# A Mamba-2 and attention layer on one core: y's norm taken for two chunks of the scan together

## Chip, cores and metric

One core of a Trainium2 chip runs the whole layer. The metric is the device time in microseconds; the time given is the median of several runs.

## What is computed

One encoder layer with two branches over 512 tokens of width 2048. After an RMSNorm and one input projection, branch A is a convolution and a bidirectional chunked state-space scan, whose result y is gated and normed in four groups of 512 columns. Branch B is attention with compressed queries and keys. Both are projected, gated, summed and projected out. Cut to what the change touches:

```python
y_fwd = ssd_scan(xs, dtf, a_f, bm, cm)                     # chunks of 128 tokens
y_bwd = flip(ssd_scan(flip(xs), flip(dtb), a_b, flip(bm), flip(cm)))
y = (y_fwd + y_bwd + d_skip[:, None] * xs)
y = y.reshape(b, s, D_SSM) * jax.nn.silu(z_ssm)
y = rmsnorm(y.reshape(b, s, SSM_GROUPS, D_SSM // SSM_GROUPS),
            ssm_norm_w.reshape(SSM_GROUPS, D_SSM // SSM_GROUPS)).reshape(b, s, D_SSM)
```

So each token has, for each of the four groups g, one root mean square over 512 columns. A chunk c is 128 tokens, one per partition; a group's chunk is a tile of 128 x 512, and its norm needs one number per partition.

## The kernel before

The kernel is one program in stages: the input's norm and transposes, the gate products (Strassen's scheme, `wz`, `wgs`, `wga`), the scan, the attention heads, and the projections. Large matmuls are done three times with fp32r halves (`mm3`, L168): a weight chunk of 128 x 1024 is loaded by SyncE (`wraw`), ScalarE (ACT) makes its high half `wh` (L164), VectorE (DVE) its low half `wl` (L165), and TensorE (PE) runs 24 matmuls from it.

The scan is `ssd_group(g)` (L1034), called for g = 0 to 3. A group has a **state loop** of three steps (L1141), which makes the running states and the off-diagonal terms `off`, and a **second loop** over four chunks c and two halves q of four heads (L1208), which makes the products within a chunk. In the second loop `seg_make` (L1170) builds the decay products G on DVE (two scans L1177, E L1180, G L1187 and L1188) and on ACT (exponential L1181, scaled copies L1186), and `diag` (L1191) lets PE multiply them into the bank `yb` (L1198). `diag` is called one half later than its G. After the second half of a chunk it adds `yb` to `yo` on DVE (L1201) and calls `y_norm` (L993).

`y_norm` multiplies by the gate z on DVE (L995), sums the squares on ACT (L997), scales the sum on DVE (L998), takes a root on ACT (L186, which needs a table load there), refines its reciprocal with five DVE operations on one column (L188 to L192, in `small_rsqrt`), and scales y by it on ACT (L999). `y_turn` (L1001) then transposes y on PE into a bank `turn` (L1005), which ACT copies out (L1009) and stores to `yn_d`.

Between these steps PE is fed from a queue of other products, `fill`: projections of the next group (`xbc`), of the attention's inputs (`qkv`) and of its gate (`za`). `gap()` (L1072) takes the next share of them, some 30 matmuls in the second loop. PE's order is the order in which the code is written; the other engines' order is set by a scheduler with priorities, and each engine runs its instructions in order. The norm has a raised priority (L1202).

Before the change, a finished chunk is put on a queue `turns`, and one is turned in each second half (q = 1) while more than one is waiting: chunk 0 at c = 2, chunk 1 at c = 3, chunk 2 at the end of the group (L1227) and chunk 3 in the first step of the next group's state loop (L1150), or for the last group after 60 matmuls of fill (L1241).

Of the kernel before, what the change touches and what calls it, by code (L numbers as in the profile page):

```python
# [12 lines left out]
F32 = mybir.dt.float32  # L13
F32R = mybir.dt.float32r
I32 = mybir.dt.int32
AF = mybir.ActivationFunctionType
ALU = mybir.AluOpType
AX = mybir.AxisListType

P = 128  # L20
# [12 lines left out]
EPS = 1e-6  # L33
# [40 lines left out]
def build(tc, a):  # L74
    nc = tc.nc
    act, dve, pool, pe = nc.scalar, nc.vector, nc.gpsimd, nc.tensor
    opened = {}

    def open_pool(name, bufs=1, side="left", **kw):
        cm = tc.tile_pool(name=name, bufs=bufs, side=side, **kw)  # L80
        p = cm.__enter__()
        opened[name] = cm
        return p
# [13 lines left out]
    hi = open_pool("hi", side="right")  # L97
# [4 lines left out]
    def few(n):  # L102

        n_small[0] += n
        assert n_small[0] <= 96
        return small[:, n_small[0] - n:n_small[0]]
# [42 lines left out]
    def pb(n="pb"):  # L149
        return ps.tile([P, SEQ], F32, tag="pb", bufs=2, name=n)  # L150

    def pc(n="pc"):
        return ps.tile([P, SEQ], F32, tag="pc", bufs=1, name=n)
# [29 lines left out]
    def small_rsqrt(v, n, new):  # L183

        t = new("rt")
        act.activation(t, v, AF.Sqrt)  # L186
        r = new("rr")
        dve.reciprocal(r, t)  # L188
        dve.tensor_mul(t, r, r)
        dve.tensor_mul(t, t, v)  # L190
        dve.tensor_scalar(t, t, -0.5, 1.5, ALU.mult, ALU.add)
        dve.tensor_mul(r, r, t)  # L192
        return r
# [12 lines left out]
    for t in range(TT):  # L206
# [3 lines left out]
        for i, cs in enumerate(slice(*e) for e in zip(edges, edges[1:])):  # L210
# [3 lines left out]
            if i == 0:  # L214
                most, v, root, r = (few(1) for _ in range(4))
# [97 lines left out]
    def put(dst, t):  # L313
        act.dma_start(dst, t)
# [113 lines left out]
    fill = Fill()  # L428
# [527 lines left out]
    def tmp2(name, n=SEQ):  # L956
        return sw.tile([P, SEQ], F32, tag="t", bufs=8, name=name)
# [14 lines left out]
    ssz = few(16)  # L972
# [8 lines left out]
                i = qkv_left.pop(0)  # L981
                fill.add("qkv", qkv_gen(i, sq_q if i < 6 else sq_kv, tmp2))

    def rsqrt1(v):

        return small_rsqrt(v, 1, lambda n: hi.tile([P, 1], F32, tag={"rt": "mx", "rr": "nm"}[n], bufs=4, name=n))

    def z_load(c, g):
        z = st("z")
        nc.sync.dma_start(z, zs_d[c][g])  # L990
        return z

    def y_norm(c, g, y, z):  # L993

        dve.tensor_mul(y, y, z)  # L995
        s_ = ssz[:, 4 * c + g:4 * c + g + 1]
        act.activation(z, y, AF.Square, accum_out=s_)  # L997
        dve.tensor_scalar(s_, s_, 1.0 / 512, EPS, ALU.mult, ALU.add)  # L998
        act.activation(y, y, AF.Copy, scale=rsqrt1(s_))  # L999

    def y_turn(c, g, y):  # L1001

        tp = pb("turn")
        for i in range(4):
            pe.transpose(tp[:, i * P:(i + 1) * P], y[:, i * P:(i + 1) * P], ident)  # L1005
        y = tmp2("yt")
        for i in range(4):
            k = 4 * g + i
            act.activation(y[:, i * P:(i + 1) * P], tp[:, i * P:(i + 1) * P], AF.Copy,  # L1009
                           scale=vec[:, V_SN + k:V_SN + k + 1] if g < 2 else vneg[:, k - 8:k - 7])  # L1010
        d = yn_d[f"x{c // 2 + 1}{g // 2 + 1}"].rearrange("p (k t) -> p k t", k=8)
        put(d[:, 4 * (g % 2):4 * (g % 2) + 4, c % 2 * P:(c % 2 + 1) * P], y.rearrange("p (k t) -> p k t", k=4))

    turns = deque()
# [19 lines left out]
    def ssd_group(g):  # L1034
# [37 lines left out]
        def gap():  # L1072
            left[0] += shares.pop(0) * left[1]
            left[0] -= fill.run(left[0])
# [54 lines left out]
        def cb_make(c):  # L1129
            cs = slice(c * P, (c + 1) * P)  # L1130
            cb = pb("cb")
            pe.matmul(cb[:, 0:P], BT[:, cs], CT[:, cs], start=True, stop=True)
            cbf = sw.tile([P, P], F32, tag="cbf", bufs=2, name="cbf")
            cbb = sw.tile([P, P], F32, tag="cbb", bufs=2, name="cbb")
            dve.tensor_mul(cbf, cb[:, 0:P], m_le)
            dve.tensor_mul(cbb, cb[:, 0:P], m_ge)
            cbs[c] = (cbf, cbb)
# [23 lines left out]
        def da_load(c, q):  # L1161
            h0 = g * HPG + q * 4
            das.append([])
            for dd in range(2):
                da = sw.tile([P, 4, P], F32, tag=f"da{dd}", bufs=2, name=f"da{dd}")
                src = da_d[dd, c, h0:h0 + 4].rearrange("h l -> (h l)")
                tc.keep_in_program_order(nc.sync.dma_start(flat(da), src.unsqueeze(0).broadcast_to([P, SEQ])))
                das[-1].append(da)

        def seg_make(c, q):  # L1170

            h0 = g * HPG + q * 4
            sums = []
            for da, mask in zip(das.popleft(), (scan_f, scan_b)):
                with tc.issue_after(put_on[0].ins) if put_on and mask is scan_b else nullcontext():
                    sums.append(tmp2("sum"))
                    dve.tensor_tensor_scan(sums[-1], flat(da), mask, 0.0, ALU.add, ALU.mult)  # L1177
            sf, sb = (t.rearrange("p (h l) -> p h l", h=4) for t in sums)
            E = sw.tile([P, 4, P], F32, tag="E", bufs=2, name="E")
            dve.tensor_add(E, sf, sb[:, :, ::-1])  # L1180
            act.activation(flat(E), flat(E), AF.Exp)  # L1181
            G = sw.tile([P, 4, P], F32, tag="G", bufs=2, name="G")
            cbf, cbb = cbs[c]
            for j in range(4):
                df, db = (dtT[:, c, o + h0 + j:o + h0 + j + 1] for o in (0, NH))
                act.activation(G[:, j], cbf, AF.Copy, scale=df)  # L1186
                dve.scalar_tensor_tensor(G[:, j], cbb, db, G[:, j], ALU.mult, ALU.add)  # L1187
            put_on[:] = [dve.tensor_mul(G, G, E)]  # L1188
            return G

        def diag(c, q, G):  # L1191

            if q == 0:
                ybs[c] = pc("yb")
            yb = ybs[c]
            for j in range(4):
                cs = slice((q * 4 + j) * 64, (q * 4 + j + 1) * 64)
                pe.matmul(yb[:, cs], G[:, j, :], xT[:, c, cs], start=True, stop=True)  # L1198
            if q == 1:
                y = sw.tile([P, SEQ], F32, tag="yz", bufs=2, name="y")  # L1200
                dve.tensor_add(y, yo[:, c], yb)  # L1201
                with tc.high_priority(offset=30):  # L1202
                    y_norm(c, g, y, zs.pop(c))
                turns.append((c, g, y))

        last = None
        da_load(0, 0)
        for c in range(TT):  # L1208
            for q in range(2):
                G = seg_make(c, q)  # L1210
                if q == 0 and c < TT - 1:
                    cb_make(c + 1)
                if (c, q) != (TT - 1, 1):
                    da_load(c + q, 1 - q)
                if q == 1:
                    zs[c] = z_load(c, g)
                gap()
                if q == 1 and len(turns) > 1:
                    y_turn(*turns.popleft())
                if last:  # L1220
                    diag(*last)
                last = (c, q, G)
# [1 line left out]
            loaded[g + 1] = group_loads(g + 1)  # L1224
        gap()
        gap()
        y_turn(*turns.popleft())  # L1227
        diag(*last)

        if g == 2:  # L1230
# [5 lines left out]
    for g in range(GROUPS):  # L1236
        ssd_group(g)
    add_fill("za", len(za_left))
    ahead[0] = 150
    fill.run(60)  # L1240
    y_turn(*turns.popleft())  # L1241
    close_pool("sw")
    close_pool("sp")
# [417 lines left out]
    def w_out(cg, kc):  # L1661
        return w_split(w_load(w_tile("w"), "wo", 0, kc // 4, cg, kc % 4))
# [42 lines left out]
    for cg in range(2):  # L1705
# [4 lines left out]
        for n, kc in enumerate(ORDER):  # L1710
            h, l = w_out(cg, kc)
# [187 lines left out]
```

## Time and profile before

| | |
|---|---|
| median of three runs | 1960.82 us (1956.30, 1960.82, 1961.52) |
| the profiled execution's own time | 1959.01 us |
| its span, first to last instruction | 1957.2 us |
| ScalarE (ACT) busy | 1038.4 us, 53% |
| GpSimd (POOL) busy | 253.0 us, 13% |
| moved by DMA | 383.29 MB, mean 196 GB/s |
| the four groups' second loops, first yb to last yb | about 630 to 691, 757 to 822, 885 to 944, 1011 to 1075 us |

PE is TensorE's matmuls, PEld its weight loads, DVE VectorE, ACT ScalarE, POOL GpSimd, SP SyncE. L12 is line 12 of the kernel before. A row of the timeline gives the start, the duration, the engine and line, the operation, the tiles (output, then inputs), and in brackets how long the engine had been idle before it and what released it. PE's matmuls overlap, so that one that lasts 0.39 us is followed by the next about 0.23 us later.

### The profile page before, as it was taken

Reading aid. Unit: us, or ns where it says so; the run is one execution under the profiler, and the core shown is the slowest. Engines: PE = TensorE matmul, PEld = TensorE weight load, DVE = VectorE, ACT = ScalarE, POOL = GpSimd, SP = SyncE. Lnnn points to the kernel's source line nnn. Section 1 sums busy time; section 2 is a strip of 40 time slices with the busy share of each in tenths; the row PEclk is TensorE's granted clock in tenths of the full one; section 3 lists DMA queues with packets and bytes.
Section 4 is the critical chain, followed back from the end, with each engine's and each line's share of the span. In section 5 each row is a group of like instructions: output and inputs, shape, how many; then the busy total and the mean of one; then the engine's idle time right before and its main releaser. Section 6 shows DMA issues by size and latency. Waiting matters only on the chain.

```text
span 1957.2 us, 24596 instructions
## 1 busy us (share of the span) xinstructions
PE 1931.4 (99%) x8874; PEld 1590.7 (81%) x8874; DVE 1462.0 (75%) x2064; ACT 1038.4 (53%) x1536; POOL 253.0 (13%) x324
## 2 busy tenths in 40 slices
PE   8999999999999999999999999999999999999998
PEld 6878888888888888888888888888877778888886
DVE  7876676776759879789786557676776889879467
ACT  7444445444465856757757444444455355454344
POOL 0011001001112030030210211111021110100011
PEclk9999999999999999999999999999999999999999
DMA  6569669668654545665544867787388787847437
GB/s 218 175 191 261 168 163 249 153 184 240 143 189 151 187 136 166 205 196 182 183 157 142 253 178 209 201 229 193 114 217 305 237 275 282 288 154 242 163 88 169
DMA packets 145306, 383.29 MB, mean 196 GB/s; under 512 B 16608, under 2 KB 34208, under 8 KB 144992
## 3 DMA queue, kind: packets, MB, share of 16 engines
q1 hardware_dynamic: 78240, 232.45, 35.6%
q0 software_dynamic: 31392, 105.40, 23.7%
q10 hardware_dynamic: 35552, 43.87, 6.3%
q8 instruction: 70, 1.15, 0.2%
q14 instruction: 52, 0.43, 0.1%
HBM read 329.55 MB, written 98.17 MB: 219 GB/s over the span
## 4 chain that ended last, share of the span: by engine, by line
PE 80%; DVE 9%; DMA 5%; issue 3%; ACT 2%; POOL 0%; SPq 0%; DVEq 0%; ACTq 0%; POOLq 0%
PE P L630 11%; PE P L631 11%; PE P L629 11%; PE za L169 3%; PE za L171 3%; PE xbc L169 3%; PE za L170 3%; PE xbc L170 3%; PE xbc L171 3%; PE qkv L171 2%; PE qkv L169 1%; PE f L1659 1%; PE f L1658 1%; PE f L1657 1%; PE qkv L170 1%
## 5 line engine op out<-in xcount | busy, mean ns | idle before, releaser
L483 ACT CAST wh<-X 128x1024 fp32r<-128x1024 f32 x164 | 172.5, 1054 | 200.6 <-PE P L631 156.9
L484 DVE TENSOR_TENSOR wl<-X,wh 128x1024 fp32r<-128x1024 f32 x164 | 199.9, 1222 | 88.7 <-ACT wh L483 88.3
L165 DVE TENSOR_TENSOR wl<-wraw,wh 128x1024 fp32r<-128x1024 f32 (+2 forms) x148 | 171.3, 1160 | 81.7 <-ACT wh L164 76.5
L164 ACT CAST wh<-wraw 128x1024 fp32r<-128x1024 f32 (+2 forms) x148 | 142.6, 967 | 113.8 <-PE za L170 31.2
L484 DVE TENSOR_TENSOR wl<-Y,wh 128x1024 fp32r<-128x1024 f32 x88 | 107.5, 1223 | 68.3 <-ACT wh L483 68.3
L483 ACT CAST wh<-Y 128x1024 fp32r<-128x1024 f32 x88 | 92.6, 1054 | 115.5 <-PE P L631 106.5
L169 PE MATMUL xbc<-h_h,wh 128*128 128x512 f32 x384 | 153.1, 399 | 0.0
L171 PE MATMUL xbc<-h_h,wl 128*128 128x512 f32 x384 | 149.9, 390 | 0.0
L170 PE MATMUL xbc<-h_l,wh 128*128 128x512 f32 x384 | 149.5, 389 | 0.0
L629 PE MATMUL P<-wh,h_h 128*128 128x512 f32 x384 | 149.4, 389 | 0.0
L630 PE MATMUL P<-wl,h_h 128*128 128x512 f32 x384 | 149.4, 389 | 0.0
L631 PE MATMUL P<-wh,h_l 128*128 128x512 f32 x384 | 149.4, 389 | 0.0
L483 ACT CAST wh<-wraw 128x1024 fp32r<-128x1024 f32 x68 | 71.7, 1054 | 112.9 <-PE P L631 64.3
L484 DVE TENSOR_TENSOR wl<-wraw,wh 128x1024 fp32r<-128x1024 f32 x68 | 83.1, 1222 | 59.6 <-ACT wh L483 59.4
L630 PE MATMUL P<-wl,S 128*128 128x512 f32 x288 | 112.3, 390 | 0.8 <-DVE wl L484 0.8
L629 PE MATMUL P<-wh,S 128*128 128x512 f32 x288 | 112.1, 389 | 0.2 <-ACT wh L483 0.2
L631 PE MATMUL P<-wh,S 128*128 128x512 f32 x288 | 112.0, 389 | 0.0
L169 PE MATMUL za<-h_h,wh 128*128 128x512 f32 x256 | 101.7, 397 | 0.0
L171 PE MATMUL za<-h_h,wl 128*128 128x512 f32 x256 | 99.9, 390 | 0.0
L170 PE MATMUL za<-h_l,wh 128*128 128x512 f32 x256 | 99.7, 389 | 0.0
L1409 ACT ACTIVATE pr<-s,nm 128x512 f32<-128x512 f32 x64 | 44.1, 689 | 79.4 <-DVE nm L1407 79.4
L171 PEld LDWEIGHTS xbc<-h_h,wl 128*128 128x128 f32 x384 | 72.1, 188 | 15.5
(754 smaller groups left out, 5101.5 us busy)
## 6 DMA issues: line engine op xcount, KB each, us to landing
wraw<-wi SPq DMA_DIRECT2D x102, 512.0 KB, 3.8
T_wps<-wps POOLq DMA_DIRECT2D x32, 512.0 KB, 11.2
da<-da_d SPq DMA_DIRECT2D x64, 256.0 KB, 3.9
T_wpa<-wpa POOLq DMA_DIRECT2D x32, 512.0 KB, 9.7
wraw<-wps SPq DMA_DIRECT2D x24, 512.0 KB, 5.9
wraw<-wo SPq DMA_DIRECT2D x20, 512.0 KB, 3.5
xbc_d<-xbc ACTq DMA_DIRECT2D x24, 256.0 KB, 2.8
wraw<-wun SPq DMA_DIRECT2D x16, 384.0 KB, 5.3
```

What stands on the lines that cost most here:

```text
L164: act.copy(h, raw)
L165: dve.tensor_sub(l, raw, h.bitcast(F32))
L169: pe.matmul(out, wh, xh, start=start, stop=False)
L170: pe.matmul(out, wh, xl, start=False, stop=False)
L171: pe.matmul(out, wl, xh, start=False, stop=stop)
L483: i = act.copy(hi_, raw)
L484: dve.tensor_sub(lo_, raw, hi_.bitcast(F32))
L629: pe.matmul(bs[i], xh, wh, start=(j == 0), stop=False)
L630: pe.matmul(bs[i], xh, wl, start=False, stop=False)
L631: pe.matmul(bs[i], xl, wh, start=False, stop=(j == 7))
L1409: act.activation(pr, s, AF.Exp, bias=nm, scale=SCALE, accum_out=sm_)
L1657: pe.matmul(acc, mh, wh, start=(start and k == 0), stop=False)
```

## The change

The odd chunk's `y_norm` now makes the norm for both chunks of a pair. The sums of squares of a group's chunks lie side by side, the even chunk's `y_norm` ends after its sum, and the odd chunk's takes one root and one set of small operations on two columns for both, then scales both tiles and puts both on `turns`. The small tiles are two fixed pairs of columns (`yr`) and no longer rotating buffers. In the second loop a chunk is turned in each second half when any is waiting, which is chunk 0 at c = 2 and chunk 1 at c = 3 as before. The turn at the end of a group is gone: chunks 2 and 3 are turned in the first and second step of the next group's state loop. For the last group the 60 matmuls of fill are cut into 42 and 18, with a turn after each.

```diff
-    def rsqrt1(v):
-        return small_rsqrt(v, 1, lambda n: hi.tile([P, 1], F32, tag={"rt": "mx", "rr": "nm"}[n], bufs=4, name=n))
+    yr = [few(2), few(2)]
...
+    halves = []
+
     def y_norm(c, g, y, z):
+        s_ = ssz[:, 4 * g + c:4 * g + c + 1]
         dve.tensor_mul(y, y, z)
-        s_ = ssz[:, 4 * c + g:4 * c + g + 1]
         act.activation(z, y, AF.Square, accum_out=s_)
-        dve.tensor_scalar(s_, s_, 1.0 / 512, EPS, ALU.mult, ALU.add)
-        act.activation(y, y, AF.Copy, scale=rsqrt1(s_))
+        halves.append((c, g, y))
+        if c % 2:
+            s2 = ssz[:, 4 * g + c - 1:4 * g + c + 1]
+            dve.tensor_scalar(s2, s2, 1.0 / 512, EPS, ALU.mult, ALU.add)
+            r = small_rsqrt(s2, 2, lambda n: yr[n == "rr"])
+            for i, h in enumerate(halves):
+                act.activation(h[2], h[2], AF.Copy, scale=r[:, i:i + 1])
+            turns.extend(halves)
+            halves.clear()
...
                 with tc.high_priority(offset=30):
                     y_norm(c, g, y, zs.pop(c))
-                turns.append((c, g, y))
...
-                if q == 1 and len(turns) > 1:
+                if q == 1 and turns:
                     y_turn(*turns.popleft())
...
         gap()
         gap()
-        y_turn(*turns.popleft())
         diag(*last)
...
-    fill.run(60)
+    fill.run(42)
+    y_turn(*turns.popleft())
+    fill.run(18)
     y_turn(*turns.popleft())
```

Three places in the order of the instructions. The first is VectorE in group 2 after chunk 0's square; `small`, `rt` and `rr` are the columns of the root, `sum`, `cbf`, `cbb` and `G` belong to the next half's products. Before:

```order
L998 TENSOR_SCALAR small<-small 128x1
L165 TENSOR_TENSOR wl<-wraw,wh 128x1024
L1177 SCALAR_TENSOR_TENSOR sum<-da_7575,scn 128x512
L1135 TENSOR_TENSOR cbf<-cb,cst 128x128
L1136 TENSOR_TENSOR cbb<-cb,cst 128x128
L188 RECIPROCAL rr<-rt 128x1
L189 TENSOR_TENSOR rt<-rr 128x1
L190 TENSOR_TENSOR rt<-rt,small 128x1
L191 TENSOR_SCALAR rt<-rt 128x1
L192 TENSOR_TENSOR rr<-rr,rt 128x1
L1188 TENSOR_TENSOR G<-G,E 128x512
```

Now, with the new kernel's line numbers (seven more from L1008 on):

```order
L165 TENSOR_TENSOR wl<-wraw,wh 128x1024
L1184 SCALAR_TENSOR_TENSOR sum<-da_7521,scn 128x512
L1142 TENSOR_TENSOR cbf<-cb,cst 128x128
L1143 TENSOR_TENSOR cbb<-cb,cst 128x128
L1195 TENSOR_TENSOR G<-G,E 128x512
```

Chunk 0's six small operations are gone from between the products. The second place is VectorE in group 3, from chunk 1's sum to the end of its root. Before:

```order
L1201 TENSOR_TENSOR y<-yo,yb 128x512
L1187 SCALAR_TENSOR_TENSOR G<-cbb,dtT,G 128x128
L995 TENSOR_TENSOR y<-y,z 128x512
L1187 SCALAR_TENSOR_TENSOR G<-cbb,dtT,G 128x128 x2
L998 TENSOR_SCALAR small<-small 128x1
L1187 SCALAR_TENSOR_TENSOR G<-cbb,dtT,G 128x128
L1188 TENSOR_TENSOR G<-G,E 128x512
L188 RECIPROCAL rr<-rt 128x1
L189 TENSOR_TENSOR rt<-rr 128x1
L190 TENSOR_TENSOR rt<-rt,small 128x1
L191 TENSOR_SCALAR rt<-rt 128x1
L192 TENSOR_TENSOR rr<-rr,rt 128x1
```

Now:

```order
L1208 TENSOR_TENSOR y<-yo,yb 128x512
L1194 SCALAR_TENSOR_TENSOR G<-cbb,dtT,G 128x128
L996 TENSOR_TENSOR y<-y,z 128x512
L1194 SCALAR_TENSOR_TENSOR G<-cbb,dtT,G 128x128 x3
L165 TENSOR_TENSOR wl<-wraw,wh 128x1024
L1195 TENSOR_TENSOR G<-G,E 128x512
L1001 TENSOR_SCALAR small<-small 128x2
L188 RECIPROCAL small<-small 128x2
L189 TENSOR_TENSOR small<-small 128x2
L190 TENSOR_TENSOR small<-small 128x2
L191 TENSOR_SCALAR small<-small 128x2
L192 TENSOR_TENSOR small<-small 128x2
```

The operations on two columns stand where those on one stood, with one split `wl` and the product G now ahead of the first of them. The third place is TensorE at the end of group 2; `rp` is the sum for the norm of the compressed keys. Before:

```order
L169 MATMUL za<-h_h,wh 128x512
L170 MATMUL za<-h_l,wh 128x512
L171 MATMUL za<-h_h,wl 128x512
L1005 MATMUL turn<-cst,y 128x128 x4
L1198 MATMUL yb<-xT,G 128x64 x4
L378 MATMUL rp<-sq_kv,cst 128x512
```

Now:

```order
L169 MATMUL za<-h_h,wh 128x512
L170 MATMUL za<-h_l,wh 128x512
L171 MATMUL za<-h_h,wl 128x512
L1205 MATMUL yb<-xT,G 128x64 x4
L378 MATMUL rp<-sq_kv,cst 128x512
```

Four transposes, chunk 2's turn, left this place; they now stand in group 3's state loop. The first turn of each group, chunk 0's, stands on TensorE where it stood.

## The prediction

> **What bounds the kernel now.** First the head of the page: the span, TensorE's and VectorE's busy time, and the clock that TensorE was granted.
>
> ```profile
> span 1957.2 us, 24596 instructions
> PE 1931.4 (99%) x8874; PEld 1590.7 (81%) x8874; DVE 1462.0 (75%) x2064; ACT 1038.4 (53%) x1536; POOL 253.0 (13%) x324
> PEclk9999999999999999999999999999999999999999
> ```
>
> TensorE is busy for all but 25.8 us. The change lies in the scan, so next the windows by stage: the four groups of the scan (560 to 1090 us), and the last stage for comparison. Columns: stretch, busy time and instructions of PE, PEld, DVE, ACT, POOL, then clock, DMA share, GB/s.
>
> ```profile
> 560.00:696.00 136.00, 136.00 (x659) 113.67 (x658) 107.44 (x176) 92.81 (x156) 20.82 (x14) 1.00 0.53 168
> 696.00:822.00 126.00, 125.44 (x604) 104.64 (x603) 102.91 (x170) 85.81 (x147) 19.72 (x14) 1.00 0.52 166
> 822.00:945.00 123.00, 120.80 (x582) 99.68 (x581) 108.30 (x179) 84.42 (x149) 20.05 (x16) 1.00 0.62 190
> 945.00:1090.00 145.00, 145.00 (x694) 120.81 (x693) 101.34 (x170) 95.68 (x163) 17.23 (x14) 1.00 0.48 149
> 1440.00:1957.00 517.00, 501.09 (x2241) 410.83 (x2239) 401.44 (x468) 247.14 (x300) 62.28 (x101) 0.99 0.69 219
> ```
>
> In the scan PE is without a gap but for 0.56 us in group 1 and 2.20 us in group 2. What it waited for there stands in the list of waits (total, times, longest):
>
> ```profile
> PE qkv L171 <- DVE wl L165: 2.1, 2, 1.6
> PE off L170 <- DVE s_l L1116: 0.6, 1, 0.6
> ```
>
> So 2.76 us is the most that relieving VectorE and ScalarE can give back in the scan, 0.14% of the time. Anything that makes PE wait there is paid in full, since PE runs its matmuls in the written order and the stages behind are full too.
>
> **What is removed.** Per pair of chunks one chain of a root and six VectorE operations on one column goes; eight chains are left of sixteen. That is 48 small operations on DVE, 0.15 us each by the rows below, 7 us; on ACT eight roots, and by the order of instructions 13 of 69 table loads, at this price:
>
> ```profile
> L186 ACT ACT_TABLE_LOAD  x16: 1283/1283/1283, 645.0 to 1078.1; - x16
> ```
>
> 13 x 1.283 = 16.7 us of ACT, which is busy 53%. Nothing on PE goes: 8297 rows before and after. As PE's matmuls cover this work, I cost the relief at nothing, except where it shortens the chain below.
>
> **What is moved: the scale of the even chunk.** Before, chunk 0 is scaled on its own, long before its transpose. In group 0, PE's product yb of chunk 1 starts between the two:
>
> ```profile
> 650.65 0.71 ACT L999 ACTIVATE y<-y,rr 128x512 f32<-128x512 f32 x1
> 653.50 1.00 PE L1198 MATMUL yb<-xT,G 128*128 128x64 f32 x8
> 660.57 0.60 PE L1005 MATMUL turn<-cst,y 128*128 128x128 f32 x4
> 661.52 0.72 ACT L999 ACTIVATE y<-y,rr 128x512 f32<-128x512 f32 x1
> ```
>
> Row one scales chunk 0, row two makes chunk 1's half, row three turns chunk 0, row four scales chunk 1. The first turn of a group keeps its place on PE. But with one root for two chunks, chunk 0 can be scaled only when chunk 1's chain has run: row four, not row one, now has to end before row three. It ends at 661.52 + 0.72 = 662.24, so PE waits 1.67 us. Behind the waiting turn PE has the other half's yb and all the projections' matmuls, and behind these the evictions.
>
> The same rows for group 1, with two DVE waits for chunk 0's chain ahead:
>
> ```profile
> 772.75 0.15 DVE L998 TENSOR_SCALAR small<-small 128x1 f32<-128x1 f32 x1 [1.53 <-ACT z L997]
> 774.55 0.16 DVE L188 RECIPROCAL rr<-rt 128x1 f32<-128x1 f32 x1 [1.16 <-ACT rt L186]
> 781.10 1.00 PE L1198 MATMUL yb<-xT,G 128*128 128x64 f32 x8
> 789.70 0.60 PE L1005 MATMUL turn<-cst,y 128*128 128x128 f32 x4
> 793.47 0.72 ACT L999 ACTIVATE y<-y,rr 128x512 f32<-128x512 f32 x1 [1.45 <-DVE rr L192]
> ```
>
> Here 794.19 - 789.70 = 4.49 us. Group 2, with the steps of the chain, and PE's own wait behind the turn:
>
> ```profile
> 906.67 1.10 PE L1198 MATMUL yb<-xT,G 128*128 128x64 f32 x8
> 911.71 0.68 DVE L1201 TENSOR_TENSOR y<-yo,yb 128x512 f32<-128x512 f32 x1
> 913.84 0.60 PE L1005 MATMUL turn<-cst,y 128*128 128x128 f32 x4
> 916.36 1.28 ACT L186 ACT_TABLE_LOAD   x1
> 919.30 0.15 DVE L188 RECIPROCAL rr<-rt 128x1 f32<-128x1 f32 x1
> 919.37 1.20 DVE L165 TENSOR_TENSOR wl<-wraw,wh 128x1024 fp32r<-128x1024 f32 x1
> 919.43 0.50 PE L171 MATMUL qkv<-h_h,wl 128*128 128x512 f32 x1 [1.57 <-DVE wl L165]
> 921.06 0.16 DVE L192 TENSOR_TENSOR rr<-rr,rt 128x1 f32<-128x1 f32 x1
> 921.25 0.73 ACT L999 ACTIVATE y<-y,rr 128x512 f32<-128x512 f32 x1 [1.45 <-DVE rr L192]
> ```
>
> 921.98 - 913.84 = 8.14 us. VectorE takes up yb only 5 us after it, because it is behind with its scans. Group 3:
>
> ```profile
> 1035.13 1.00 PE L1198 MATMUL yb<-xT,G 128*128 128x64 f32 x8
> 1042.87 0.60 PE L1005 MATMUL turn<-cst,y 128*128 128x128 f32 x4
> 1043.27 0.72 ACT L999 ACTIVATE y<-y,rr 128x512 f32<-128x512 f32 x1
> ```
>
> 1043.99 - 1042.87 = 1.12 us. With chunk 1's chain as it was, the sum is 1.67 + 4.49 + 8.14 + 1.12 = 15.42 us.
>
> **Corrections to it.** Group 2's later wait of 1.57 us for wl is covered by the new one, since VectorE goes on meanwhile: -1.57. In group 1 DVE no longer waits 1.53 + 1.16 = 2.69 us for chunk 0's chain; part of it stays, as the products G that stand between wait for ACT themselves, so I take -1.2, of 0 to -2.69. In group 2 DVE is full, and only the six small operations' 6 x 0.15 = 0.9 us goes from ahead of chunk 1: -0.7, of 0 to -0.9. In group 3 one more split wl (1.20 us in the row of group 2) stands ahead of the pair's root than before, and in group 0 one stands ahead of chunk 1's sum; DVE has idle time for part: +0.8 and +0.7, of 0 to 1.2 each. Sum: 15.42 - 1.57 - 1.2 - 0.7 + 0.8 + 0.7 = 13.45 us. The second copy that scales chunk 1 comes behind the first and no turn waits for it.
>
> **The last turns.** The third turn of a group moves from its end into the next group's state loop, and takes the fourth's old place there; the fourth moves one step on. What hides the pair's chain is the next group's first projections, as for the fourth now, in group 1's rows:
>
> ```profile
> 835.85 0.72 ACT L999 ACTIVATE y<-y,rr 128x512 f32<-128x512 f32 x1
> 844.21 0.60 PE L1005 MATMUL turn<-cst,y 128*128 128x128 f32 x4
> ```
>
> 844.21 - 836.57 = 7.64 us to spare: nothing. Without that cover it would cost as much as a first turn. In the last group the third turn comes after 42 matmuls of fill:
>
> ```profile
> 1074.20 1.00 PE L1198 MATMUL yb<-xT,G 128*128 128x64 f32 x8
> 1081.49 0.72 ACT L999 ACTIVATE y<-y,rr 128x512 f32<-128x512 f32 x1
> 1088.73 0.60 PE L1005 MATMUL turn<-cst,y 128*128 128x128 f32 x4
> ```
>
> 60 matmuls took 14.53 us, so 42 take about 10.2 and the turn falls at 1084.4, 2.2 us after the scale's end at 1082.21: nothing. The moved turn's store is late too, and POOL copies what it stores; that is a rival below. SP's loads of da, z and wraw change places by one or two with each other; no row of before has PE waiting for them.
>
> **Rivals.** *The chain is quicker than before's rows say* (slower, but by little). If it takes in each group what it takes in group 0, 662.24 - 653.50 = 8.74 us from yb to the scaled y, the waits are 4 x 8.74 less the four distances from yb to turn, 7.07 + 8.60 + 7.17 + 7.74 = 30.58: 4.38 us, less 1.57: +2.8 us, 1961.8 us. For it: two table loads fewer ahead of it on ACT and DVE's 2.69 us. Against: groups 1 and 2 run 13.1 and 15.3 us, and most of that is VectorE's own work. This case spans 1961.8 to about 1967.
>
> *It ends no slower.* If the chain comes under 7.07 us, the shortest distance, no turn waits, and the 2.1 us of waits for wl may go: 1959.01 - 2.1 = 1956.9 us. It decides at these 7.07 us. Against: no row here is below 8.74.
>
> *More is lost.* POOL's copy of yn for the second operand waits for a store that now leaves one state step later, and POOL is in order: sums yo stand behind it.
>
> ```profile
> 865.52 0.51 POOL L1447 DMA_DIRECT2D yn_S<-yn_S  x1 [11.48 <-DMA yn_S<-yn_x]
> ```
>
> It waits 11.48 us already, with no wait on PE over 0.6 us near it; about 12 us more holds two temporaries that VectorE's scans need next. And PE's clock may fall in a long wait: no idle piece of PE here passes 1.6 us in the scan and the clock stays at 1.00, so no row prices it; half speed for as long as group 2's wait would cost some 3.5 us more. With the uncorrected 15.42, both wl in full (+2.4) and this, 1959.01 + 15.42 + 2.4 + 3.5 = 1980.3; 1974 to 1980.
>
> The Trainium skill, TensorE: Matmul & The Clock Gate, section "The HAM clock gate", says that TensorE's clock drops to half after an idle window of about 3.4 us and needs about as long a busy one to return. By that rule group 2's wait would cost an estimated 1.7 us more, and the sum would be 1974.1 us; no run here shows it yet.
>
> **How the numbers follow.** The profiled execution took 1959.01 us, 1.81 more than its span, and lies 1.81 below the median of 1960.82; I make the sum against it: 1959.01 + 13.4 = 1972.4 us. The forecast (turn waits of 8 to 16 us) gets 0.66, the quicker chain 0.20, more loss 0.10, no slower 0.04. The range reaches from the quicker chain's 1962 to 1979, short of the worst sum. A measurement of this kernel tells about 0.3% (5.9 us) from no change: below 1966.7 counts as same. Slower by more: 0.66 + 0.10 = 0.76. Same: the quicker chain and half of the last rival, 0.22. Faster: 0.02, as there are only 2.76 us to win in the scan.
>
> **What would show it.** After, each group's first turn should be preceded by an idle PE released by ACT's scale of y: about 2.5, 3, 7 and 2 us, with the wl wait behind group 2's gone, and 48 small DVE rows and 13 table loads fewer. The page's chain should run through ACT and DVE ahead of these turns. It is wrong if PE has no wait at the turns, if the waits sum to under 8 us, or if the time comes from elsewhere, as the state loops of groups 1 to 3.

## The result, and the profile after

The changed kernel takes 1986.01 us (median of 4 runs, 1982.77 to 1987.00), the kernel before 1960.30 us beside it (4 runs): ratio 1.0137, 95% interval 1.0125 to 1.0149. It is slower, by 25.7 us where 11.6 were forecast, and lies above the range of 1962 to 1979 us. The profiled execution took 1987.0 us; against the one of before (1959.01) that is 28.0 us, and the spans differ by the same.

The head of the page of after: the span, TensorE's row, and the granted clock in 40 slices.

```profile
span 1985.2 us, 24521 instructions
PE 1942.7 (98%) x8874; PEld 1598.4 (81%) x8874; DVE 1458.4 (73%) x2016; ACT 1021.3 (51%) x1515; POOL 252.4 (13%) x324
PEclk9999999999999999998999999999999999999999
```

PE runs the same 8874 matmuls but is busy 11.3 us longer (1931.4 before). Its idle time grew from 25.8 to 42.5 us, by 16.7. So the 28.0 us are two things, waiting and slower matmuls, and only the first was in the forecast's sum. DVE lost its 48 small operations and ACT 21 instructions, with 3.6 and 17.1 us of busy time; PE got nothing from that.

The windows of the four groups of the scan, same columns and same times as before, though the changed kernel comes later by up to 19 us at the end of the scan (stretch, PE, PEld, DVE, ACT, POOL, clock, DMA share, GB/s):

```profile
560.00:696.00 136.00, 133.67 (x637) 111.63 (x636) 104.59 (x161) 84.26 (x142) 20.75 (x14) 0.99 0.49 162
696.00:822.00 126.00, 122.78 (x577) 102.28 (x576) 100.96 (x160) 80.75 (x144) 19.06 (x13) 0.97 0.50 153
822.00:945.00 123.00, 114.82 (x531) 94.15 (x530) 103.39 (x158) 74.21 (x130) 20.44 (x17) 0.96 0.56 181
945.00:1090.00 145.00, 142.32 (x683) 117.99 (x682) 100.66 (x157) 90.63 (x156) 16.71 (x13) 1.00 0.48 153
```

Every group has idle PE now, and the clock, 1.00 in all four before, is 0.96 to 0.99 in three of them. What PE waited for in the scan, and in the 87 us behind the last turn, by the list of waits (total, times, longest; `loc` and `off` are products of the state loop, `za` the gate's and `vp` the values' projection behind the scan):

```profile
PE turn L1012 <- ACT y L1004: 14.7, 4, 7.6
PE loc L170 <- DVE xw_l L1107: 1.1, 1, 1.1
PE off L170 <- DVE s_l L1123: 0.5, 1, 0.5
...
PE vp L1349 <- ACT wh L164: 0.9, 1, 0.9
PE za L171 <- DVE wl L165: 0.8, 1, 0.8
PE vp L1350 <- DVE wl L165: 0.8, 1, 0.8
PE za L169 <- ACT wh L164: 0.5, 1, 0.5
```

The first row is the four first turns, as forecast. The waits for wl in the projections (2.1 us) are gone, as forecast too. The last four rows, 3.0 us behind the scan, stand where before has no wait at all. Sum: 14.7 + 1.1 + 0.5 + 3.0 less the former 2.1 + 0.6 is 16.6 us, the growth of idle time.

The first turn of each group, with the product yb behind it in groups 2 and 3 (start, duration, in brackets the idle time ahead):

```profile
663.07 0.84 PE L1012 MATMUL turn<-cst,y 128*128 128x128 f32 x4 [2.33 <-ACT y L1004]
796.45 1.08 PE L1012 MATMUL turn<-cst,y 128*128 128x128 f32 x4 [3.22 <-ACT y L1004]
932.18 1.12 PE L1012 MATMUL turn<-cst,y 128*128 128x128 f32 x4 [7.59 <-ACT y L1004]
933.09 1.81 PE L1205 MATMUL yb<-xT,G 128*128 128x64 f32 x8
1066.19 0.66 PE L1012 MATMUL turn<-cst,y 128*128 128x128 f32 x4 [1.53 <-ACT y L1004]
1066.68 1.00 PE L1205 MATMUL yb<-xT,G 128*128 128x64 f32 x8
```

Behind the wait of 7.59 us the four transposes take 1.12 us and the eight products 1.81; behind 1.53 us, 0.66 and 1.00. The windows of 4 us behind the turns of groups 0, 1, 2 and 3 show why, in the clock (the column after POOL's, 1.00 at full speed):

```profile
663.00:667.00 4.00, 3.93 (x17) 3.60 (x18) 4.00 (x3) 3.55 (x9) 1.76 (x1) 0.57 0.53 188
797.00:801.00 4.00, 4.00 (x16) 3.61 (x15) 4.00 (x8) 3.78 (x11) 0.00 (x0) 0.50 0.34 99
801.00:805.00 4.00, 4.00 (x14) 3.14 (x14) 2.09 (x3) 2.01 (x3) 1.27 (x1) 0.71 0.52 181
932.00:936.00 4.00, 3.81 (x15) 3.62 (x16) 3.27 (x4) 2.86 (x9) 0.00 (x0) 0.50 0.75 257
936.00:940.00 4.00, 4.00 (x11) 3.05 (x10) 2.77 (x5) 2.05 (x7) 0.00 (x0) 0.51 0.68 203
1066.00:1070.00 4.00, 3.81 (x23) 3.38 (x24) 4.00 (x4) 3.69 (x10) 0.00 (x0) 1.00 0.53 167
```

After three of the four waits PE runs at half clock with nothing to wait for. The record of the clock in the trace has these stretches: 3.41 us from 663.41, 6.83 us from 796.53 and 10.24 us from 929.65, of which PE still waits for 2.54. So PE works for 17.9 us at half clock and loses half of that, 9.0 of the 11.3 us. Another 3.41 us at half clock stand at 1636.21, in the last stage, where the trace of before has none: 1.7 us more.

### The profile page after: what moved, and what is told of

It is laid out like the page before. It is cut to its first block, busy times and chain, and to the rows that moved or that the text cites. A ratio compares the mean times of both kernels' runs of the same rounds, so it can differ in the third digit from the quotient of the medians.

```text
span 1985.2 us, 24521 instructions
## 1 busy us (share of the span) xinstructions
PE 1942.7 (98%) x8874; PEld 1598.4 (81%) x8874; DVE 1458.4 (73%) x2016; ACT 1021.3 (51%) x1515; POOL 252.4 (13%) x324
## 4 chain that ended last, share of the span: by engine, by line
PE 41%; DVE 5%; DMA 4%; issue 2%; ACT 1%; POOL 1%; SPq 0%; POOLq 0%; DVEq 0%; ACTq 0%
PE P L630 4%; PE P L631 4%; PE P L629 4%; PE za L169 2%; PE za L170 2%; PE za L171 2%; PE f L1664 1%; PE f L1665 1%; PE f L1666 1%; PE pb L1429 1%; PE qp L171 1%; PE qp L169 1%; PE qp L170 1%; DMA wraw<-wps 1%; DMA yn_S<-yn_x 1%
```

## The experiments

The theory was that the first turns wait for the joint chain and that half clock follows; the rival, that the moved turns of the last group are the main cost. Three questions were asked in turn: the first turns and the clock (runs 1 to 4), what is lost behind the scan (5 to 7, 9 to 12), and when the clock falls (8). A ratio is to the kernel before, in the same series of runs, with its 95% interval. A diff is from the changed kernel, or from the kernel that the text names; `...` marks code left out.

### 1. The first two turns later

```diff
-                if q == 1 and turns:
+                if c == 3 and turns:
```

> The changed kernel with chunks 0 and 1 turned in the two halves of c = 3, so the first turn comes two gaps (about 15 us) and not one (about 7.5 us) behind chunk 1's yb. Theory 1, the loss is TensorE's wait at the first turn of each group (14.7 us) and the half clock behind it (about 8.5 us): the four waits are gone or under 1 us in sum, no clock below 1.00 in the scan, 1957 to 1964 us. Rival, the loss comes from the two turns moved into the next group's state loop, with their stores and the loads queued behind: no change, 1975 to 1987 us.

Measured: 1965.98 us, ratio 1.0037 (1.0025 to 1.0049), 2 us above the interval of theory 1. No turn waits, and the clock stays at 1.00 through the scan. So 20 of the 25.7 us go with the waits of the first turns. Some 6 us stay. Behind the scan PE again waits for weights of za and vp, 3.9 us in sum.

### 2. Only the first pair

Chunks 0 and 1 share a root; chunks 2 and 3 keep their own, and all turns stand as before.

```diff
+        if c > 1:
+            dve.tensor_scalar(s_, s_, 1.0 / 512, EPS, ALU.mult, ALU.add)
+            act.activation(y, y, AF.Copy, scale=rsqrt1(s_))
+            turns.append((c, g, y))
+            return
...
```

> Chunks 0 and 1 normed together, chunks 2 and 3 each by itself; all turns where the kernel before has them. Theory 1: all the loss is here, turn waits of 14 to 16 us with half clock behind three of them, 1980 to 1987 us. Rival, the moved last turns are the cause: 1958 to 1965 us.

Measured: 1983.06 us, ratio 1.0124 (1.0110 to 1.0139); turn waits of 2.32, 3.22, 6.23 and 1.53 us. The first pair alone makes nearly the whole loss; the rival of the moved last turns falls as the main cause. But here too PE waits 3.5 us for za behind the scan, with no turn moved there, and a stretch of 6.83 us at half clock begins in that wait.

### 3. Only the last pair

Chunks 2 and 3 share a root, with the moved turns; 0 and 1 are single, with their turns as before.

```diff
+        if c < 2:
+            dve.tensor_scalar(s_, s_, 1.0 / 512, EPS, ALU.mult, ALU.add)
+            act.activation(y, y, AF.Copy, scale=rsqrt1(s_))
+            turns.append((c, g, y))
+            return
...
-                if q == 1 and turns:
+                if q == 1 and c > 1 and turns:
```

> Chunks 0 and 1 each by itself, chunks 2 and 3 normed together and turned in the next group's state loop as in the changed kernel, 42 and 18 matmuls of fill in the last group. Theory 1: no wait at a first turn, 1957 to 1964 us. Rival, the moved last turns are the cause: 1970 to 1985 us.

Measured: 1965.21 us, ratio 1.0029 (1.0016 to 1.0042), between the two intervals. No wait at a turn. The second pair and what is moved with it cost nearly 6 us: PE waits for za and vp behind the scan (3.9 us), and one stretch of 3.41 us at half clock follows.

### 4. The waits filled with spare matmuls

```diff
                 if q == 1 and turns:
+                    if c == 2:
+                        spare = pa("spare")
+                        for _ in range((10, 14, 33, 6)[g]):
+                            pe.matmul(spare, h_h[:, 0, :P], h_h[:, 0, :], start=True, stop=True)
                     y_turn(*turns.popleft())
```

> The changed kernel with 10, 14, 33 and 6 extra matmuls of 128x512 into an unused bank ahead of the first turn of groups 0 to 3 (2.3, 3.2, 7.5 and 1.4 us at 0.227 us each), so that TensorE works while it would wait. The extra matmuls are no part of the result. Theory 1 with the clock: the delay of about 14.7 us stays, but the clock keeps 1.00 behind the turns, so about 8.5 us less than the changed kernel: 1975 to 1979 us. Rival, the clock's drop costs nothing by itself and the time behind the turns is lost for another reason: 1984 to 1988 us.

Measured: 1975.95 us, ratio 1.0090 (1.0074 to 1.0106). The matmuls do no useful work and the turns come no earlier, yet the kernel is 10.1 us faster than the changed one: the clock stays at 1.00 in all the windows shown above. PE's busy time, 1948.8 us, less 63 spare matmuls of 0.23 us is 1934.3, 8.4 us less than in the changed kernel. Half clock costs 8 to 10 us, as the 9.0 us from the record of the clock have it. The other 10.0 us down to run 1 are the waits themselves: 14.5 us of spare matmuls, less 1.9 us of a wait for wl that run 1 has and these hide, less 2.3 us by which run 1 waits longer behind the scan, 10.3 us.

### 5, 6, 7. What is lost behind the scan

In run 1, ACT's copies yt of the moved third turn stand ahead of a weight cast wh, and what SP loads behind that comes 3.3 us late. Theory A says that this is the rest of the loss; theory B that the loads there collide in any order but that of before.

Run 5: run 1 with both last turns behind 60 matmuls.

```diff
-    fill.run(42)
-    y_turn(*turns.popleft())
-    fill.run(18)
+    fill.run(60)
     y_turn(*turns.popleft())
+    y_turn(*turns.popleft())
```

> The turn-later kernel (turns of chunks 0 and 1 at c == 3) with one change: both of the last group's turns stand behind fill.run(60), not one behind 42 and one behind 60. What is in dispute is the 6 us that the turn-later kernel still loses. Theory A, the moved turn stands in ACT's row: in the turn-later trace ACT waits 2.46 us for the moved turn's transposes at 1085.84 and the cast wh that stood at 1085.98 in the trace of before comes at 1089.27; wl, a weight load on SP and then the loads of R and raw, which are queued behind it, follow 3.3 us late (R at 1092.01 instead of 1088.74), into a stretch where the DMA engines are full, and the weights of vp come 6 us late. With both turns behind 60 the cast stands ahead of them again: R is back at about 1089, the 3.8 us of waits for za and vp between the last turn and 1165 go down to under 1, time 1959.5 to 1962.5. Theory B, the loads behind the scan collide whatever the turn does, because the tail's order came out otherwise: the waits stay, 1964 to 1967.

Run 6: the kernel before, with nothing paired, and its last third turn moved.

```diff
-        y_turn(*turns.popleft())
+        if g < GROUPS - 1:
+            y_turn(*turns.popleft())
         diag(*last)
...
-    fill.run(60)
+    fill.run(42)
+    y_turn(*turns.popleft())
+    fill.run(18)
     y_turn(*turns.popleft())
```

> The kernel before with its norms and its other turns untouched; only the last group's third turn is moved from the end of the group to behind fill.run(42). Theory A (the moved turn's place in ACT's row delays a weight cast, and with it the loads behind the scan): ACT waits about 2.5 us for the moved turn, R is issued at about 1092, 3 to 4 us of PE waits for za and vp follow: 1962 to 1965. Theory B (the pairing's change of the tail's order does it): as before, 1958.5 to 1960.5.

Run 7: run 1 with the last group's norms single and its turns as in the kernel before.

```diff
+        if g == GROUPS - 1:
+            dve.tensor_scalar(s_, s_, 1.0 / 512, EPS, ALU.mult, ALU.add)
+            r = small_rsqrt(s_, 1, lambda n: yr[n == "rr"][:, c % 2:c % 2 + 1])
+            act.activation(y, y, AF.Copy, scale=r)
+            turns.append((c, g, y))
+            return
...
```

> The turn-later kernel with the last group as in the kernel before: its four norms single, its third turn at the end of the group and its fourth behind fill.run(60); pairs in groups 0 to 2 alone, their turns of chunks 0 and 1 at c == 3. Theory A (only the moved turn of the last group costs): no waits behind the scan, 1959 to 1961.5, no difference from before, since neither the first turns wait nor anything is moved behind the scan. Theory B (the loads behind the scan collide in any order but that of before; the kernel with the first pairs alone had 3.6 us of waits for za there with no turn moved): 1962.5 to 1966.

Measured: run 5, 1966.85 us, ratio 1.0041 (1.0028 to 1.0053); run 6, 1962.83 us, 1.0024 (1.0016 to 1.0033); run 7, 1960.81 us, 1.0007 (0.9999 to 1.0016). Runs 6 and 7 are as theory A has them: moving one turn of the unpaired kernel costs 4 us, and pairs with nothing moved behind the scan cost nothing that can be told. Run 5 lies in the interval of theory B: the cast came in time there, but one load of wi more stands ahead of R on SP, R goes out only at 1097.24, and the waits (3.4 us) stay. So it is not the cast as such.

The mechanism in rows. First the kernel before, ACT's rows behind the scan:

```profile
1085.98 1.05 ACT L164 CAST wh<-wraw 128x1024 fp32r<-128x1024 f32 x1 [3.76 <-PE za L170]
1087.05 1.28 ACT L455 ACT_TABLE_LOAD   x1
1088.35 0.60 ACT L455 ACTIVATE za<-za 128x512 f32<-128x512 f32 x1
1089.37 1.14 ACT L1009 ACTIVATE yt<-turn,small 128x128 f32<-128x128 f32 x4 [0.42 <-PE turn L1005]
```

Run 6, the same place:

```profile
1084.94 1.14 ACT L1009 ACTIVATE yt<-turn,small 128x128 f32<-128x128 f32 x4 [3.07 <-PE turn L1005]
1086.85 1.28 ACT L455 ACT_TABLE_LOAD   x1 [0.77 <-ACT yt L1009]
1088.15 0.60 ACT L455 ACTIVATE za<-za 128x512 f32<-128x512 f32 x1
1088.64 1.04 ACT L164 CAST wh<-wraw 128x1024 fp32r<-128x1024 f32 x1
```

The cast comes at 1088.64 instead of 1085.98. VectorE makes wl from it, only then is the raw weight's buffer free for SP's next load, and R (the norm's factors of the compressed queries) and the raw activations are queued behind that load. SP's rows, before:

```profile
1088.74 0.38 SPq L1261 DMA_DIRECT2D R<-rq_d  x1
1089.18 5.05 SPq L1264 DMA_DIRECT2D raw<-qkv_d  x6
1122.01 5.89 SPq L161 DMA_DIRECT2D wraw<-wv  x2
```

and in run 6:

```profile
1091.39 0.38 SPq L1264 DMA_DIRECT2D R<-rq_d  x1
1091.82 4.61 SPq L1267 DMA_DIRECT2D raw<-qkv_d  x6
1126.62 6.49 SPq L161 DMA_DIRECT2D wraw<-wv  x2
```

R is 2.65 us late and the weights wv 4.6. The last casts wh for za stand behind those of raw on ACT, which wait for raw, and so are late as well. PE waits 3.2 us for za and vp.

### 8. Part of the waits filled

Run 4 with fewer spare matmuls.

```diff
-                        for _ in range((10, 14, 33, 6)[g]):
+                        for _ in range((0, 6, 24, 0)[g]):
```

> The changed kernel with 0, 6, 24 and 0 spare matmuls (128x512, about 0.23 us each, into a bank that nobody reads) ahead of the first turns of groups 0 to 3, so that the idle time left ahead of them is about 2.3, 1.8, 2.1 and 1.5 us instead of 2.3, 3.2, 7.6 and 1.5. It measures from which idle time the granted clock falls. If it falls only from somewhere above 2.1 us: group 0 alone shows half clock behind its turn, about 1.7 us over the kernel with spare matmuls throughout (1975.95), so 1976.5 to 1979. If already 1.8 us is enough: groups 0, 1 and 2 all show it, 1.7 to 3.4 us each, 1980 to 1984.

Measured: 1981.83 us, ratio 1.0117 (1.0102 to 1.0133), between the two cases. The first turns and their idle time:

```profile
663.07 0.66 PE L1012 MATMUL turn<-cst,y 128*128 128x128 f32 x4 [2.31 <-ACT y L1004]
794.85 0.66 PE L1012 MATMUL turn<-cst,y 128*128 128x128 f32 x4 [1.86 <-ACT y L1004]
928.78 1.09 PE L1012 MATMUL turn<-cst,y 128*128 128x128 f32 x4 [2.18 <-ACT y L1004]
1062.35 0.66 PE L1012 MATMUL turn<-cst,y 128*128 128x128 f32 x4 [1.53 <-ACT y L1004]
```

The time lies in the second interval, but the clock did as neither case says: it fell after 1.86 and 2.18 us and not after 2.31, though in the changed kernel it fell after 2.33. So the length of the wait alone does not decide it.

The record of the clock shows what does. In all fourteen traces, from the first rise to full clock to the last fall behind the kernel's end, every stretch at one clock is a whole number of steps of 3.413 us: one, two and three for the changed kernel's half clocks, 193 ahead of the first, 570 for the kernel before. The first rise comes at 4.53 to 7.40 us of the span, so the steps are not tied to the kernel's start. Cut at these steps, run 8 reads as follows (stretch, PE's busy time, then the other engines, clock, DMA):

```profile
659.19:662.60 3.41, 1.57 (x7) 0.95 (x6) 2.21 (x11) 3.40 (x7) 0.00 (x0) 1.00 0.60 213
662.60:666.02 3.42, 2.95 (x19) 2.69 (x20) 3.42 (x4) 3.27 (x9) 1.79 (x1) 1.00 0.29 93
792.31:795.72 3.41, 1.55 (x11) 1.09 (x11) 3.27 (x10) 2.33 (x5) 0.00 (x0) 1.00 0.69 244
795.72:799.13 3.41, 3.41 (x12) 2.93 (x12) 3.41 (x7) 3.25 (x10) 0.00 (x0) 0.50 0.30 87
925.43:928.84 3.41, 1.23 (x7) 0.69 (x6) 3.38 (x7) 3.09 (x5) 0.00 (x0) 1.00 0.77 241
928.84:932.25 3.41, 3.41 (x15) 3.22 (x16) 2.98 (x4) 2.30 (x7) 0.00 (x0) 0.50 0.81 253
```

The wait of 2.31 us lies across an edge, with 1.84 us of it in one step and 0.47 in the next, and the clock stays. The waits of 1.86 and 2.18 us lie in one step each, and the clock falls at its end. It is so in all fourteen traces: the clock fell behind every step at full clock in which PE was idle for 1.86 us or more (28 of them, with those at the kernels' ends), and behind none with 1.84 us or less. So it goes by how much of a wait falls into one step. That is why a wait of about 2 us can go either way: by the 2.0 us for wl in run 11 the clock fell for 3.41 us, and by the 1.95 us for the same wl in run 1, across an edge, it did not. Why it then lasts one step, two or three the traces do not show.

### 9, 10. The moved turn three matmuls earlier

Behind 39 matmuls instead of 42, the cast stands right behind yt and ahead of the table load. Run 9 is run 1 with that, run 10 is run 6 with it.

```diff
-    fill.run(42)
+    fill.run(39)
     y_turn(*turns.popleft())
-    fill.run(18)
+    fill.run(21)
```

> The turn-later kernel with the last group's third turn three fill matmuls earlier, behind 39 instead of 42, and the fourth behind 21 more. In ACT's order of instructions the cast wh then stands right behind the moved turn's copies yt, ahead of the table load and of za, where with 42 it stood behind all of them; SP's order is the same as with 42 (two loads wi behind the first six raw). Theory A, sharpened after the kernel with both turns behind 60 (there the cast came on time, and R was still late because one load wi more stood ahead of it on SP): what counts is when SP gets to R, and with the cast back at about 1087 R is issued at 1089 to 1090, the waits for za and vp between the last turn and 1165 go down from 3.8 us to under 1, and the time is that of the kernel with the last group single, 1959.5 to 1962.5. Theory B (the loads behind the scan collide whatever SP does): the waits stay, 1964 to 1967.

> The kernel before with only the last group's third turn moved, as in the run with fill.run(42), but behind 39 and 21. ACT's order again has the cast wh right behind the moved turn's copies, ahead of the table load. Theory A: R is issued at about 1089, no wait over 0.5 us behind the scan, 1958 to 1960.5, no difference from before, where behind 42 it took 1962.83. Theory B (the moved turn costs wherever it stands behind the scan): 1962 to 1964.

Measured: run 10, 1958.46 us, ratio 0.9998 (0.9989 to 1.0007), against 1.0024 behind 42: theory A holds for the unpaired kernel. Run 9 missed it: 1967.72 us, 1.0041 (1.0029 to 1.0054), no better than run 1. R is in time, the second raw load is not. SP's rows of run 9:

```profile
1089.83 0.38 SPq L1268 DMA_DIRECT2D R<-rq_d  x1
1090.27 0.42 SPq L1271 DMA_DIRECT2D raw<-qkv_d  x1
1097.53 0.32 SPq L1271 DMA_DIRECT2D raw<-qkv_d  x1
```

ACT's queue and the landing of the stores of yt, in run 9:

```profile
1091.63 0.38 ACTq L314 DMA_DIRECT2D yn_x<-yt  x1
...
DMA to landing us min/median/max: 2.2/4.0/5.8
```

1091.63 + 5.8 = 1097.43, and the second raw load goes out at 1097.53. In the compiled order this load waits for ACT and for that store, where in the kernel before it does not:

```
before: L1264 DMA raw<-qkv_d_118 128x512 [waits DMAHW7_49,DMAHW3_49,Pool_49]
run 9:  L1271 DMA raw<-qkv_d_118 128x512 [waits DMAHW7_49,DMAHW4_49,Activation_49]
```

The pool behind the scan reuses the scan's memory, and in run 9 the last yt lies under a buffer of raw. The same gap shows in the changed kernel and in runs 1 and 2 (4.3, 4.3 and 7.7 us from one raw load to the next). It comes with a pair in the last group and not with the moved turn: run 2 has it with no last turn moved; run 7, with the last group single, has its first six raw loads at most 1.5 us apart; and run 10, with the turn moved and nothing paired, goes from the first raw load to the second in 0.53 us.

### 11, 12. R and raw on other memory

Run 11 is run 9 with R and raw placed first in their pool; run 12 is the kernel before with the same, to price the placement by itself.

```diff
+    for tag, n in (("R", 2), ("raw", 6)):
+        for _ in range(n):
+            aw.tile([P, SEQ], F32, tag=tag, bufs=n, name=f"{tag}_place")
     k1, k2 = (aw.tile([P, SEQ], F32, tag="a", bufs=6, name=n) for n in ("k1", "k2"))
```

> The turn-later kernel with 39 and 21 fill matmuls, and the tiles R and raw placed first in their pool, so that they lie on other memory. What the last two kernels left: behind 39, R was issued in time (1089.83), but the second raw load only at 1097.53, 7.3 us after the first; in the compiled order that load waits for ACT and for the store of the last turn's yt, which was issued at 1091.63 and landed 5.8 us later: the buffer of raw lies where that yt lay. The kernel with the first pairs alone (third raw load 7.7 us late), the turn-later kernel (4.3) and the changed kernel (4.3) show the same gap, the kernel before none. Here no raw load waits for ACT or that store (the loads of k on the GpSimd queue do instead). Theory A2 (two delays on SP's way to wv: the cast behind the moved turn, and raw's buffer under the last yt): six raw loads within 5 us, waits for za and vp behind the scan under 0.5 us, 1959.5 to 1962. Theory B (the loads collide there whatever SP does): waits of 3 us or more stay, 1964 to 1968.

> The kernel before with R and raw placed first in their pool and nothing else, as the measure for the kernel with raw first: there the raw loads already go out within 5 us and PE has no wait between 1090 and 1200, so theory A2 expects no difference, 1957.5 to 1960.5. If the placement itself gains or loses (k's loads now wait for the last yt's store), it shows here; theory B, by which any other order of these loads costs, expects 1962 or more.

Measured: run 11, 1962.27 us, ratio 1.0013 (1.0004 to 1.0023); run 12, 1960.55 us, 1.0008 (0.9998 to 1.0017). The six raw loads of run 11:

```profile
1092.52 3.44 SPq L1271 DMA_DIRECT2D raw<-qkv_d  x6
1107.95 8.94 SPq L161 DMA_DIRECT2D wraw<-wur  x2
1121.97 6.49 SPq L161 DMA_DIRECT2D wraw<-wv  x2
```

wv is issued at 1121.97, 6.3 us earlier than in run 1, and PE has no wait between 1090 and 1300. Theory A2, two delays on SP's way to the weights, holds; its median lies 0.3 us above the expected interval. Theory B falls, as run 12's other order costs nothing that can be told, though PE waits 1.1 us for vp there.

## Why the prediction failed

The sign was right and the size was not: 13.6 us lie between 1972.4 and 1986.0. The ratios of four kernels take the loss apart, each step undoing one thing:

| kernel | ratio | the step, of 1960 us |
|---|---|---|
| changed | 1.0137 | |
| waits filled, clock kept (run 4) | 1.0090 | half clock: 0.0047, 9.2 us |
| first turns later (run 1) | 1.0037 | waits of the first turns: 0.0053, 10.4 us |
| and the loads behind the scan in time (run 11) | 1.0013 | late loads behind the scan: 0.0024, 4.7 us |

With the intervals of the ratios, each step is good to 0.0015 to 0.0020, which is 3 to 4 us.

- **PE bounds the scan, and relief is worth nothing: right.** Run 11 has all of the change's savings on DVE and ACT (1456.3 and 1019.8 us busy against 1462.0 and 1038.4) and is not faster than before.
- **The turn waits: right in place and size.** "About 2.5, 3, 7 and 2 us" were 2.33, 3.22, 7.59 and 1.53, where the corrected rows give 2.37, 3.29, 7.44 and 1.92 group by group: the mechanism held in each. The projections' waits for wl went with them. (The page counts 8874 matmuls in both kernels, where the prediction writes 8297 rows; that nothing goes on PE holds.)
- **The clock: this step failed.** The prediction put it into a rival of 0.10 because "no row prices it", and gave it 3.5 us, for group 2 only, as half speed "for as long as group 2's wait". Measured it is 8 to 10 us in three groups. The time at half clock does not follow the wait: 3.22 us bought 6.83 us of work at half clock, and 7.59 us bought 7.70. The prediction's own rows had three waits longer than any idle piece of before (1.6 us). That no row priced the clock there was a reason to widen the range, and was read as a reason to leave the term out. The Trainium skill, TensorE: Matmul & The Clock Gate, section "Part 1: The HAM clock gate (the "warmup" mystery)", has the clock halved after an idle window of about 3.4 us and calls the window free-running. By the first, only group 2's wait would count, and the estimate of 1.7 us was made from it. The traces agree on the window: every stretch between changes of the clock is a multiple of 3.413 us, and the first change is not tied to the kernel's start. They differ on how idle it must be: 1.86 us of idle PE within one window were enough (run 8), and 1.84 were not.
- **The moved last turns, "nothing": this step failed too.** The question asked was whether PE would wait at the turn, and it does not. What was left out is what stands behind the turn. Its copies stand in ACT's row ahead of a weight cast, and that alone costs 4 us in run 6 without any pairing. And with a pair in the last group the last store of yt holds memory that the next stage loads into, whether a turn is moved or not (run 2). In the changed kernel's trace PE waits 3.0 us for both, and the table has 4.7 us for them.
- **The rival of POOL's copies of yn** was not tried by itself. Runs 7 and 11 keep the turns that moved into the state loops, and their ratios are worth 1.4 and 2.5 us in all; in the state loops only a wait of 1.2 us for loc shows that before hasn't.
- **The sum.** Its own term held: 13.4 us forecast for the waits of the turns, 12.6 by the trace (14.7 less the 2.1 of wl), 10.4 by the ratios, in a step where run 1 waits 2.3 us longer behind the scan. The ratio of 1.0137 is 26.9 us; the table's three steps make 24.3 of it, 14 of them from the two terms that were set to nothing, and 2.5 us stay in run 11. The two profiled executions close too: of their 28.0 us, 16.6 are waits (12.6 at the turns, 3.0 behind the scan, 1.0 in the state loops) and 11.3 longer matmuls, 10.7 of them by the record of the clock.

What stays open: why run 5's compiled order has one load more ahead of R, why the half clock lasts one step of 3.41 us behind one wait and two or three behind another, and what the 2.5 us of run 11 are (in its profiled execution, 1.2 us of a wait for loc and 1.7 us by a stretch at half clock). No version here beats the kernel before; run 7 cannot be told from it, and run 11 is 0.13% slower.

## What to carry to other kernels

Batching a small chain with its neighbour's takes work off the engines, but the first half now waits for the second: look where its result is due, and move the consumer with it (run 1), or the saving turns into a wait. On a saturated PE a wait of about 2 us and more is to be priced with half clock behind it, which lost 1.7 to 3.9 us each time in the changed kernel's scan, or filled with other matmuls. When a step is moved, ask of every instruction that it issues what stands behind it on its own engine's queue, and what later tile lies on the memory that it holds.

## What the runs showed of the hardware

- PE's granted clock changes in steps of 3.413 us. It fell to 0.50 behind every step with 1.86 us or more of idle PE and behind none with 1.84 or less, in fourteen traces; within the changed kernel's scan it then stayed there for 3.41, 6.83 and 10.24 us.
- Spare matmuls in place of a wait made the kernel 10 us faster with no useful work done earlier.
- In run 9 one store of 5.8 us, 1091.63 to 1097.43, held back SP's loads for 7.3 us through shared memory, and PE felt it only 23 us later, by a wait of 2.6 us for wl that ended at 1123.44.
